# A ring of four tiles for the divided weights in a hybrid mixer block, in place of two tiles set aside for one pair

## The chip, the cores and the metric

The kernel runs on one core of one Trainium2 chip. The metric is the device time of one execution in microseconds, the median of several runs. Names of engines: PE is TensorE (PEld its weight loads, which may overlap with the matmuls), DVE is VectorE, ACT is ScalarE, POOL is GpSimd, and SP issues most of the DMAs.

## The reference

One block for 512 tokens of width 1024: a norm, one wide projection, four sequence mixers side by side, gates, an output projection, and a feed-forward part with a short convolution. Everything is float32.

```python
D_MODEL = 1024; SEQ = 512; MIX_WIDTH = 512; D_FF = 2816
u = rms_norm(h, mix_norm_g[l])
fa, fb, fc, fd, fg = _split(u @ w_in[l], MIXER_IN_SIZES)
branches = (rwkv7_mix(fa, ...), gla_mix(fb, ...), mlstm_mix(fc, ...), ssd_mix(fd, ...))
gates = jax.nn.sigmoid(fg).reshape(bsz, t, N_BRANCH, D_MODEL)
merged = gates[:, :, 0] * (branches[0] @ branch_proj[l, 0])
for i in range(1, N_BRANCH):
    merged = merged + gates[:, :, i] * (branches[i] @ branch_proj[l, i])
h = h + merged @ w_out[l]
u = rms_norm(h, ffn_norm_g[l])
gate, val = _split(causal_dwconv(u @ ffn_up[l], ffn_conv_w[l], ffn_conv_b[l]), (D_FF, D_FF))
h = h + (jax.nn.silu(gate) * val) @ ffn_down[l]
return rms_norm(h, final_norm_g)
```

Of the four mixers, `rwkv7_mix` is a recursion with a matrix state of 64x64 per head, `gla_mix` a gated linear attention with 4 heads, `mlstm_mix` a gated attention with a convolution ahead of it, and `ssd_mix` a state space model in chunks of 128 tokens.

## The kernel before

**Dense work.** A float32 operand is divided into a part `hi` that TensorE takes at its fast rate (type F32R) and the rest, `lo`. A product is three matmuls: `hi` by `hi`, `hi` by `lo`, `lo` by `hi` (`mm3`, lines L232 to L234; L327 to L329 where tokens are the output's rows). Activations are divided once (`uh`, `ul` and their like). Weights come from HBM in halves of 128x512 (`raw`, three tiles). For each half ACT copies `raw` to `hi` (L222), and DVE or, for some, POOL subtracts to get `lo` (L223). Both parts live in rings of three tiles each (`w_tiles`, L215, pool `wp`). Each output tile of 128x512 collects eight blocks of 128 in PSUM, from a ring of three (`psd`); an L899, for instance, reads it for the convolution of mLSTM, in three steps by the three earlier tokens, and the last one frees the tile.

**Mixers.** Between the dense matmuls stand the small ones of the mixers, in plain float32: L810, L821, L835, L847, L851 of the gated linear attention (L821 makes the chunks' contributions to the state, 64x128 from 32 rows; L835 the scores within a chunk, 32x32 from 64 rows), L626 to L687 of the rwkv recursion, L1002 to L1060 of the state space model. In the rwkv part, DVE inverts triangular matrices of 32x32 in 31 steps of two instructions (`Mt` L597, `Mi` L599), twice in the program (two halves of heads); the result goes to DRAM and comes back in another layout as `MN` and `MT` (L600 to L613). L626 needs `MN`, L631 needs `MT`; then eight chunks follow one another through L650, L661, L663 (DVE), L673, L687 (TensorE) and the state `st` (DVE).

**The feed-forward part.** `fm_halves` computes two output tiles at once, one of the gate and one of the value, from four halves of weights. The weights of the first pair are wanted while the last work of the part before still goes on. Three of its four halves use the rings, the fourth two tiles of their own, `wxh` and `wxl`, in a pool `hw` that is closed right after.

**What sets the order.** The code is written stage by stage, but the order on each engine is set by the framework: a list scheduler goes through all instructions with a model of their times, and takes at each point what is ready by that model, by a priority. `split_h` gives the divide a raised priority (`tc.high_priority`). A tile of a ring counts as free once its last reader is done, so the number of tiles decides when a divide counts as ready, and with that what comes next on every engine. After that the order is fixed; on the chip each engine takes its instructions in that order and waits on semaphores.

Of the kernel before, what the change touches and what calls it, by code (L numbers as in the profile page):

```python
# [10 lines left out]
F32R = mybir.dt.float32r  # L11
# [5 lines left out]
P = 128  # L17
# [143 lines left out]
def kernel(ctx: ExitStack, tc: tile.TileContext, A, out):  # L161
# [22 lines left out]
    wp = ctx.enter_context(tc.tile_pool(name="wp", bufs=1))  # L184
# [7 lines left out]
    def pd():  # L192
        return dense[0].tile([P, T], F32, tag="d", name="psd")
# [18 lines left out]
        return pf[lo:hi, PF_AT[name] + i:PF_AT[name] + i + 1]  # L212

    def w_tiles():
        return (wp.tile([P, 512], F32R, tag="hi", name="hi", bufs=3), wp.tile([P, 512], F32R, tag="lo", name="lo", bufs=3))  # L215

    def split_h(src, h, tiles=None, eng=V):
        raw = wp.tile([P, 512], F32, tag="raw", name="raw", bufs=NRAW)
        nc.sync.dma_start(raw, src[:, 512 * h:512 * h + 512])
        hi, lo = tiles or w_tiles()  # L220
        with tc.high_priority(Q["split"]):
            S.copy(hi, raw)  # L222
            eng.tensor_tensor(lo, raw, hi.bitcast(F32), op=ALU.subtract)  # L223
        return hi, lo
# [3 lines left out]
    def split_w(src, tiles=(None, None), eng=V):  # L228
        return [split_h(src, h, tiles[h], G if (pl[0] >> h) & 1 else eng) for h in range(2)]

    def mm3(ps, lh, ll, rh, rl, first, last):
        PE.matmul(ps, lh, rh, start=first, stop=False)  # L232
        PE.matmul(ps, lh, rl, start=False, stop=False)  # L233
        PE.matmul(ps, ll, rh, start=False, stop=last)  # L234
# [36 lines left out]
    def fm_halves(jobs, eng=V):  # L271
        ws = [split_w(src, tiles, eng) for src, tiles in jobs]
        pss = [pd() for _ in jobs]
        for h in range(2):
            ts = slice(256 * h, 256 * h + 256)
            for w, ps in zip(ws, pss):
                for k in range(KD):
                    hi, lo = w[k // 4]
                    ks = slice((k % 4) * P, (k % 4 + 1) * P)
                    mm3(ps[:, ts], hi[:, ks], lo[:, ks], uh[:, k, ts], ul[:, k, ts], k == 0, k == KD - 1)  # L280
        return pss
# [919 lines left out]
    nc.sync.dma_start(gb2, A["gvec"][D:2 * D].partition_broadcast(P))  # L1201
    gb3 = hp.tile([P, D], F32, name="gb3")
    nc.sync.dma_start(gb3, A["gvec"][2 * D:3 * D].partition_broadcast(P))
    hw_ctx = ExitStack()
    hw = hw_ctx.enter_context(tc.tile_pool(name="hw", bufs=1, side="right", reuse_waits="tile"))
    wx = [hw.tile([P, 512], F32R, name=n) for n in ("wxh", "wxl")]
    hx = ExitStack()
    np_ = hx.enter_context(tc.tile_pool(name="nq", bufs=1, side="right", reuse_waits="tile"))

# [18 lines left out]
        norm_T(h2[:, b], gb2, b, np_, uh, ul, 1, [pr_, pm])  # L1228
    tap("h2", h2)
    hx.close()  # L1230
    first = fm_halves([(A["up"][0], (None, None)), (A["up"][1], (None, (wx[0], wx[1])))])
    hw_ctx.close()
    wo_ctx.close()
    mo_ctx.close()
    ps_ctx.close()
# [91 lines left out]
```

## Time and profile before

| | us |
|---|---|
| Median of 3 runs | 1225.39 |
| Lowest and highest run | 1217.79, 1230.0 |
| Profiled execution, its own time | 1220.7 |
| Its span, first to last instruction | 1218.9 |
| TensorE busy in it (share of span) | 1166.5 (96%) |
| VectorE, ScalarE, GpSimd busy | 653.7, 445.5, 333.1 |
| Mean granted clock of TensorE | 0.981 |

Busy times are sums over the span. A busy TensorE is not a TensorE at its peak: a matmul's record reaches from its start to a modelled end, and neighbours overlap. Where records overlap, the distance from start to start tells what an instruction takes of the engine. A matmul in plain float32 leaves two records.

### The profile page before, as it was taken

The page shows a single profiled execution, that of the slowest core. Times are in us where ns is not written, and L with a number is a line of the kernel's source. Part 1 is how long each engine was busy: PE and PEld are TensorE (multiplying, and loading weights), DVE is VectorE, ACT ScalarE, POOL GpSimd, SP SyncE. Part 2 cuts the span into 40 slices and gives each one's busy share as a digit, 9 for nine tenths or more (in the row PEclk, how much of TensorE's full clock was granted, in tenths as well). Part 3 has the DMA queues.
Part 4 walks back from the last instruction along what each step waited for, and adds up shares of the span by engine and source line. Part 5 has one row for each costly group of instructions (what it writes and reads, how often), then busy time and mean ns, then how long its engine had stood idle before and what let it go on. Part 6 is the DMA issues. An engine that isn't in the chain of part 4 may idle for free.

```text
span 1218.9 us, 17897 instructions
## 1 busy us (share of the span) xinstructions
PE 1166.5 (96%) x6881; PEld 935.6 (77%) x6881; DVE 653.7 (54%) x1090; ACT 445.5 (37%) x820; POOL 333.1 (27%) x287
## 2 busy tenths in 40 slices
PE   5999989999999998989999999999999999999997
PEld 4886865777779965767877877778888888888886
DVE  5257792444675437397224654464556656562323
ACT  4355232223322533223123434342444444442323
POOL 3113110023473246241112363440122222220100
PEclk9998987999999999999999999999999999999999
DMA  5122330122332221323123532463222322323232
GB/s 203 62 88 65 83 85 25 36 83 83 97 104 70 95 90 65 81 78 109 60 72 105 190 112 87 164 217 87 79 95 95 103 96 96 95 95 100 92 102 104
DMA packets 79886, 117.30 MB, mean 96 GB/s; under 512 B 22660, under 2 KB 27172, under 8 KB 79800
## 3 DMA queue, kind: packets, MB, share of 16 engines
q1 hardware_dynamic: 79224, 115.11, 29.7%
q8 instruction: 54, 0.88, 0.3%
q10 hardware_dynamic: 576, 1.05, 0.2%
q14 instruction: 32, 0.26, 0.1%
HBM read 107.93 MB, written 8.19 MB: 95 GB/s over the span
## 4 chain that ended last, share of the span: by engine, by line
PE 74%; DVE 10%; DMA 7%; issue 4%; POOL 2%; ACT 2%; SPq 0%; POOLq 0%; DVEq 0%; ACTq 0%
PE psd L232 16%; PE psd L233 16%; PE psd L234 15%; PE psd L1276 3%; PE psd L1274 3%; PE psd L1275 3%; DVE Mt L597 2%; DVE Mi L599 2%; PE psd L328 2%; PE psd L327 2%; PE psd L329 2%; DVE lo L223 2%; DMA sab<-ad 2%; PE psr L673 1%; DMA raw<-in_wo_dram 1%
## 5 line engine op out<-in xcount | busy, mean ns | idle before, releaser
L223 DVE TENSOR_TENSOR lo<-raw,hi 128x512 fp32r<-128x512 f32 x280 | 226.7, 811 | 299.9 <-ACT hi L222 285.0
L222 ACT CAST hi<-raw 128x512 fp32r<-128x512 f32 x322 | 199.4, 620 | 495.6 <-PE psd L233 300.7
L232 PE MATMUL psd<-uh,hi 128*128 128x512 f32 (+1 forms) x912 | 364.0, 400 | 15.0 <-ACT hi L222 5.1
L234 PE MATMUL psd<-uh,lo 128*128 128x512 f32 (+1 forms) x912 | 362.7, 398 | 5.4 <-DVE lo L223 4.2
L233 PE MATMUL psd<-ul,hi 128*128 128x512 f32 (+1 forms) x912 | 360.5, 396 | 0.2 <-DVE ul L249 0.2
L232 PEld LDWEIGHTS psd<-uh,hi 128*128 128x128 f32 x912 | 173.3, 190 | 57.0 <-ACT hi L222 7.3
L234 PEld LDWEIGHTS psd<-uh,lo 128*128 128x128 f32 x912 | 173.4, 190 | 48.8 <-DVE lo L223 6.2
L233 PEld LDWEIGHTS psd<-ul,hi 128*128 128x128 f32 x912 | 173.4, 190 | 37.3 <-issue 3.1
L223 POOL TENSOR_TENSOR lo<-raw,hi 128x512 fp32r<-128x512 f32 x42 | 57.1, 1360 | 245.8 <-ACT hi L222 176.0
L1263 POOL TENSOR_TENSOR y<-y 128x512 f32<-128x512 f32 x22 | 28.3, 1288 | 172.3 <-DVE y L1257 158.4
L1257 DVE SCALAR_TENSOR_TENSOR y<-psd,pf,y 128x510 f32<-128x510 f32 x88 | 65.8, 749 | 3.0 <-issue 0.3
L1276 PE MATMUL psd<-hi,al 128*128 128x512 f32 x164 | 63.8, 389 | 0.0
L1275 PE MATMUL psd<-lo,ah 128*128 128x512 f32 x164 | 63.8, 389 | 0.0
L1274 PE MATMUL psd<-hi,ah 128*128 128x512 f32 x164 | 57.3, 389 | 0.0
L328 PE MATMUL psd<-lo,uh 128*128 128x256 f32 x192 | 56.1, 292 | 1.0 <-DVE lo L223 1.0
L327 PE MATMUL psd<-hi,uh 128*128 128x256 f32 x192 | 55.5, 289 | 0.0
L329 PE MATMUL psd<-hi,ul 128*128 128x256 f32 x192 | 55.4, 289 | 0.0
L328 PEld LDWEIGHTS psd<-lo,uh 128*128 128x128 f32 x192 | 37.0, 193 | 5.0 <-issue 3.2
L327 PEld LDWEIGHTS psd<-hi,uh 128*128 128x128 f32 x192 | 36.9, 192 | 1.9 <-issue 1.3
L329 PEld LDWEIGHTS psd<-hi,ul 128*128 128x128 f32 x192 | 37.0, 193 | 1.3 <-issue 1.0
L1275 PEld LDWEIGHTS psd<-lo,ah 128*128 128x128 f32 x164 | 30.8, 188 | 6.4
L1276 PEld LDWEIGHTS psd<-hi,al 128*128 128x128 f32 x164 | 30.8, 188 | 6.4
(418 smaller groups left out, 1725.6 us busy)
## 6 DMA issues: line engine op xcount, KB each, us to landing
raw<-in_wfm_dram SPq DMA_DIRECT2D x140, 256.0 KB, 2.6
raw<-in_up_dram SPq DMA_DIRECT2D x88, 256.0 KB, 2.5
raw<-in_dn_dram SPq DMA_DIRECT2D x44, 256.0 KB, 2.5
raw<-in_bp_dram SPq DMA_DIRECT2D x32, 256.0 KB, 2.6
raw<-in_wtm_dram SPq DMA_DIRECT2D x24, 256.0 KB, 2.6
raw<-in_wo_dram SPq DMA_DIRECT2D x16, 256.0 KB, 2.7
gd<-th SPq DMA_DIRECT2D x15, 256.0 KB, 2.1
th<-gd SPq DMA_DIRECT2D x15, 256.0 KB, 3.0
```

What stands on the lines that cost most here:

```text
L222: S.copy(hi, raw)
L223: eng.tensor_tensor(lo, raw, hi.bitcast(F32), op=ALU.subtract)
L232: PE.matmul(ps, lh, rh, start=first, stop=False)
L233: PE.matmul(ps, lh, rl, start=False, stop=False)
L234: PE.matmul(ps, ll, rh, start=False, stop=last)
L327: PE.matmul(o, uh[:, k, bs], hi[:, cs], start=first, stop=False)
L328: PE.matmul(o, uh[:, k, bs], lo[:, cs], start=False, stop=False)
L329: PE.matmul(o, ul[:, k, bs], hi[:, cs], start=False, stop=last)
L1257: V.scalar_tensor_tensor(y[:, d:T], ps[:, 0:T - d], col("fcw", k * 44 + n), y[:, d:T], op0=ALU.mult, op1=ALU.add)
L1274: PE.matmul(ps, ah[:, k, bs], hi, start=(k == 0), stop=False)
L1275: PE.matmul(ps, ah[:, k, bs], lo, start=False, stop=False)
L1276: PE.matmul(ps, al[:, k, bs], hi, start=False, stop=(k == NF - 1))
```

## The change

The two rings get four tiles each, and the pool `hw` goes; the fourth half of the first up pair takes its tiles from the rings like the others.

```diff
     def w_tiles():
-        return (wp.tile([P, 512], F32R, tag="hi", name="hi", bufs=3), wp.tile([P, 512], F32R, tag="lo", name="lo", bufs=3))
+        return (wp.tile([P, 512], F32R, tag="hi", name="hi", bufs=4), wp.tile([P, 512], F32R, tag="lo", name="lo", bufs=4))
...
-    hw_ctx = ExitStack()
-    hw = hw_ctx.enter_context(tc.tile_pool(name="hw", bufs=1, side="right", reuse_waits="tile"))
-    wx = [hw.tile([P, 512], F32R, name=n) for n in ("wxh", "wxl")]
     hx = ExitStack()
...
-    first = fm_halves([(A["up"][0], (None, None)), (A["up"][1], (None, (wx[0], wx[1])))])
-    hw_ctx.close()
+    first = fm_halves([(A["up"][0], (None, None)), (A["up"][1], (None, None))])
```

No instruction that computes is added or removed. The scheduler's order changes on all engines from the first mixers on. TensorE's dense matmuls stand in the same order among themselves; the small ones stand at other places between them. Groups of small matmuls between dense ones were 189 and are 141.

TensorE, before, in the gated linear attention of its second pair of heads (`psm_2026` and `psm_2027` are two PSUM tiles that L821 fills, `psd_2276` is a dense output tile):

```order
L821 MATMUL psm_2027<-w_1424,w_1907 64x128
L233 MATMUL psd_2276<-ul_85,hi_2272 128x512
L821 MATMUL psm_2026<-w_1425,w_1907 64x128
L234 MATMUL psd_2276<-uh_84,lo_2273 128x512
L821 MATMUL psm_2027<-w_1425,w_1907 64x128
L232 MATMUL psd_2276<-uh_84,hi_2272 128x512
L821 MATMUL psm_2026<-w_1425,w_1907 64x128
L233 MATMUL psd_2276<-ul_85,hi_2272 128x512
L821 MATMUL psm_2027<-w_1425,w_1907 64x128
```

TensorE, after, the same L821 (`MT` is that of the recursion):

```order
L631 MATMUL psr<-MT,Y_926 32x32 x31
L650 MATMUL psr<-vp_615,zm_710 64x64 x3
L673 MATMUL psr<-vp_615,zm_710 64x64 x8
L821 MATMUL psm<-w 64x128 x10
L687 MATMUL psr<-xs,MT 64x64
L821 MATMUL psm<-w 64x128 x4
L687 MATMUL psr<-xs,MT 64x64 x3
L650 MATMUL psr<-vp_615,zm_710 64x64 x4
L821 MATMUL psm<-w 64x128 x2
```

The single L821 between dense matmuls now stand together with steps of the recursion, and no dense matmul is between them.

TensorE, before, some 6 us of dense work later (`psm_2060` and `psm_2061` are filled by L835):

```order
L835 MATMUL psm_2060<-w_1909,w_1910 32x32
L232 MATMUL psd_2321<-uh_84,hi_2311 128x512
L835 MATMUL psm_2061<-w_1909,w_1910 32x32
L233 MATMUL psd_2321<-ul_85,hi_2311 128x512
L835 MATMUL psm_2060<-w_1909,w_1910 32x32
L234 MATMUL psd_2321<-uh_84,lo_2312 128x512
L835 MATMUL psm_2061<-w_1909,w_1910 32x32
L232 MATMUL psd_2321<-uh_84,hi_2317 128x512
```

TensorE, after, the same L835:

```order
L234 MATMUL psd<-uh,lo 128x512
L673 MATMUL psr<-uu,zm_710 64x64 x8
L673 MATMUL psr<-vp_615,zm_710 64x64 x8
L835 MATMUL psm<-w 32x32 x29
L661 MATMUL psr<-st,kr 64x64 x4
L835 MATMUL psm<-w 32x32 x3
L232 MATMUL psd<-uh,hi 128x512
```

All 32 L835 of these two tiles moved into one gap between dense matmuls.

VectorE, before, in the first inverse, where the third L899 (128x511) frees a dense PSUM tile:

```order
L223 TENSOR_TENSOR lo_2183<-raw_2180,hi_2182 128x512
L599 TENSOR_TENSOR Mi_845<-Mi_845,Mt_846 64x10x22
L899 SCALAR_TENSOR_TENSOR w_2166<-psd_2141,pf_77,w_2166 128x509
L597 TENSOR_TENSOR Mt_846<-Ls_842,Mi_845 64x207
L899 SCALAR_TENSOR_TENSOR w_2166<-psd_2141,pf_77,w_2166 128x510
L599 TENSOR_TENSOR Mi_845<-Mi_845,Mt_846 64x9x23
L827 SCALAR_TENSOR_TENSOR w_1779<-w_1778,gdk_1690,w_1779 128x128
L899 SCALAR_TENSOR_TENSOR w_2166<-psd_2141,pf_77,w_2166 128x511
```

VectorE, after, the same place:

```order
L223 TENSOR_TENSOR lo_2183<-raw_2180,hi_2182 128x512
L599 TENSOR_TENSOR Mi_845<-Mi_845,Mt_846 64x12x20
L899 SCALAR_TENSOR_TENSOR w_2166<-psd_2141,pf_77,w_2166 128x509
L597 TENSOR_TENSOR Mt_846<-Ls_842,Mi_845 64x231
L899 SCALAR_TENSOR_TENSOR w_2166<-psd_2141,pf_77,w_2166 128x510
L599 TENSOR_TENSOR Mi_845<-Mi_845,Mt_846 64x11x21
L223 TENSOR_TENSOR lo_2228<-raw_2225,hi_2227 128x512
L899 SCALAR_TENSOR_TENSOR w_2166<-psd_2141,pf_77,w_2166 128x511
```

The third L899 stands behind four steps of the inverse fewer, and the `lo` of the next weight half has come ahead of it.

## Rows read from the trace of the kernel before

**Rows 1.** The page: busy time by engine, and the granted clock in 40 slices.

```profile
PE 1166.5 (96%) x6881; PEld 935.6 (77%) x6881; DVE 653.7 (54%) x1090; ACT 445.5 (37%) x820; POOL 333.1 (27%) x287
...
PEclk9998987999999999999999999999999999999999
```

**Rows 2.** Waits of PE: who waits, for what, us, times, longest.

```profile
PE psd L232 <- ACT hi L222: 5.1, 4, 1.8
PE psd L232 <- DVE w L899: 5.0, 1, 5.0
PE psd L234 <- DVE lo L223: 4.2, 4, 2.5
PE psm L1048 <- DVE sab L1044: 2.4, 1, 2.4
...
PE psr L626 <- DMA MN<-mnd: 1.5, 1, 1.5
...
PE psd L234 <- POOL lo L223: 1.2, 2, 0.8
```

**Rows 3.** Windows: length, busy of PE, PEld, DVE, ACT, POOL; clock, DMA share, GB/s.

```profile
179.20:229.50 50.30, 50.30 (x453) 28.98 (x452) 18.69 (x40) 12.36 (x23) 3.81 (x3) 0.80 0.14 37
179.20:207.20 28.00, 28.00 (x289) 15.81 (x288) 6.73 (x13) 6.72 (x13) 1.52 (x2) 0.74 0.15 37
...
930.00:960.00 30.00, 30.00 (x134) 24.86 (x133) 19.28 (x23) 13.80 (x22) 7.74 (x6) 1.00 0.29 97
324.80:379.10 54.30, 50.18 (x269) 42.43 (x268) 42.17 (x78) 15.39 (x33) 38.65 (x32) 0.97 0.34 94
130.70:174.50 43.80, 38.73 (x299) 31.75 (x298) 42.36 (x102) 14.29 (x26) 7.48 (x5) 0.92 0.19 62
```

**Rows 4.** Lines of PE from 179.2 to 229.5: busy, mean ns, idle.

```profile
L234 PE MATMUL psd<-uh,lo 128*128 128x512 f32 x21 | 11.6, 552 | 0.0
...
L821 PE MATMUL psm<-w 32*64 32x128 f32 x64 | 10.9, 329 | 0.0
L835 PE MATMUL psm<-w 64*32 64x32 f32 x64 | 6.2, 204 | 0.0
```

**Rows 5.** Timeline of PE, L835 in turns: start, duration, instruction.

```profile
211.88 0.25 PE L835 MATMUL psm<-w 64*32 64x32 f32 x2
212.05 0.50 PE L233 MATMUL psd<-ul,hi 128*128 128x512 f32 x1
212.49 0.24 PE L835 MATMUL psm<-w 64*32 64x32 f32 x2
```

**Rows 6.** Timeline of PE, L821 in turns, at full and half clock.

```profile
190.49 0.43 PE L821 MATMUL psm<-w 32*64 32x128 f32 x2
...
191.28 0.43 PE L821 MATMUL psm<-w 32*64 32x128 f32 x2
...
195.38 0.69 PE L821 MATMUL psm<-w 32*64 32x128 f32 x2
...
196.72 0.68 PE L821 MATMUL psm<-w 32*64 32x128 f32 x2
```

**Rows 7.** Timeline of PE, the same two lines in rows.

```profile
146.13 1.10 PE L821 MATMUL psm<-w 32*64 32x128 f32 x32
...
154.18 0.94 PE L835 MATMUL psm<-w 64*32 64x32 f32 x64
```

**Rows 8.** Timeline of PE, L673 at half clock and at full.

```profile
202.69 1.12 PE L673 MATMUL psr<-uu,zm 64*64 64x64 f32 x16
203.60 1.06 PE L673 MATMUL psr<-vp,zm 64*64 64x64 f32 x16
204.60 0.79 PE L233 MATMUL psd<-ul,hi 128*128 128x512 f32 x1
...
221.69 0.63 PE L673 MATMUL psr<-vp,zm 64*64 64x64 f32 x16
222.26 0.25 PE L835 MATMUL psm<-w 64*32 64x32 f32 x2
```

## The prediction

> **What bounds the kernel now.** First the busy times of the page: TensorE (PE) is busy for 1166.5 of 1218.9 us, the next engine for about half [rows 1]. So the end is set by PE's row of work, and a time can change in only two ways: PE waits less or more, or the same matmuls take another time. Second, what PE waits for [rows 2]. The change gives the divided weights one more tile, so the waits for `hi` and `lo` are what it could take away directly: 5.1 + 4.2 + 1.2 = 10.5 us. That is the bound for the obvious effect, under one per cent.
>
> Third, the windows [rows 3]. From 930 to 960 us PE does 134 matmuls in 30.00 us, 0.224 each, at a clock of 1.00 and with no gap. That is what a dense matmul (128x512, lines L232 to L234) costs when nothing disturbs it; there a fourth tile has nothing to give. From 179.20 to 229.50 PE counts as fully busy too, yet it gets through only 61 dense matmuls (21, and 20 for each of the other two lines) and a few hundred small ones [rows 4]. 61 x 0.224 is 13.7 us; the other 36.6 us go to matmuls of 32 and 64 rows and columns (each has two records, so the 64 of L835 are 32 instructions), and to a clock that is 0.74 on average up to 207.2.
>
> The timeline shows why. One L835 and one dense matmul take turns, and each pair takes 212.49 - 211.88 = 0.61 us [rows 5]; less the dense 0.224 that is 0.38 for one L835. Where 32 L835 stand in a row, all of them take 0.94 us, 0.03 each [rows 7]. For L821 a turn takes 191.28 - 190.49 = 0.79 us at full clock and 196.72 - 195.38 = 1.34 at half clock [rows 6], so 0.57 and 1.12 beside the dense; sixteen in a row take 1.10 [rows 7], 0.07 each. What is paid is the alternation.
>
> **A rule weighed against these rows.** The Trainium skill, "Perfetto Trace Analysis", section Identifying the Most-Contended Engine, says that the busy share of matmuls is no good measure of TensorE and that the busy share of weight loads is better. The rows agree: by matmul time the stretch has no idle time and nothing could be won in it, but weight loads are busy for 28.98 of its 50.30 us against 24.86 of 30.00 in the steady one [rows 3]. By the first view the gain there is 0; by the second the stretch, at the steady share, would take 28.98 / 0.829 = 35.0 us, a gain of 15.3. The count of instructions below, which does without this rule, gives somewhat more.
>
> **The change, part by part.** No operation is added or removed: the two extra tiles go, the ring has the same four for the first up pair, and the casts are as many. What the extra tile does before that is to move places, since the scheduler may set a divide earlier. PE's dense matmuls keep their order; the small ones move.
>
> *L835.* In the order of before the 32 of `psm_2060`/`psm_2061` stand one by one between dense matmuls, but for nine; in the new one as 29 and 3. By the timeline 22 gaps hold one L835 alone, so 22 x 0.38 = 8.4 us; in a row these 22 cost 22/32 x 0.94 = 0.7. Gain 7.7.
>
> *L821.* Of the 32 in the stretch, twelve are already together, and 16 stand alone or in twos in 14 gaps: seven at full clock, 7 x 0.57 = 4.0, and seven at half clock, 7 x 1.12 = 7.8, together 11.8. In a row sixteen cost 1.10. Gain 10.7. The seven at half clock rest on the clock's staying up in the new order; if it falls there too, about 7 x 0.5 = 3.5 of it are lost.
>
> *Three gaps with L821 and steps of the recursion* (L687, L650, L673). The 16 L673 of one of them take 204.60 - 202.69 = 1.91 us at half clock; at full clock eight of them take 222.26 - 221.69 = 0.57, so all 1.14 [rows 8]: 0.8. The three L821 in them are worth 0.57 to 1.12 each. 2.5 to 4 in all; I take 3.
>
> Together 21.4 us, with bounds of 17 (the clock still falls, the mixed gaps at their low end) and 22.5.
>
> *New waits in the packed rows.* L687 now has only small matmuls between itself and L631, on which it depends through a copy on ACT; L661 has 29 L835 (0.9 us) between itself and the DVE steps that make `st`. The nearest waits of PE are those of [rows 2], 1 to 2.5 us and once 5.0; there are some seven such dependent steps, most with dense work before them. 0 to 6 us; I take 3, nearer to the cover in the order than to the worst row.
>
> *Weight waits.* 10.5 us at most [rows 2]. `raw` keeps three tiles, and ACT and DVE still serve other chains, so a fourth tile helps only where a divide can start earlier and its engine is free. The long one is a `lo` that stands behind steps of the inverse (`Mt`/`Mi`) on DVE, and the new order sets such a `lo` some steps earlier. Bounds -10.5 to +4 (other places can wait instead); I take -2.
>
> *L899.* PE waits 5.0 us for the third L899, which frees the PSUM tile [rows 2]; the PSUM ring is unchanged. In the new DVE order that L899 stands behind four steps of the inverse fewer, while a second `lo` has come ahead of it. A DVE instruction there takes 42.36/102 = 0.42 us on average [rows 3], so 4 x 0.42, less a little: -1.5, with bounds 0 and -5.0.
>
> *The inverse.* With three more L899 in its midst the first chain ends some 4 us later, and its first user L626 stands 5.2 us of dense work later (23 x 0.224): nothing. The second chain has the same, and PE already waits 1.5 us for `MN` behind it [rows 2]: +1, bounds -1.5 to +3.
>
> *The SSD stage.* It comes 22 us of dense work later and has other dense work between its groups: 33 matmuls of half the size where 24 full ones stood, 3.7 us of cover in place of 5.4. PE idles there now for 54.30 - 50.18 = 4.1 us [rows 3], of it 2.4 at L1048 [rows 2]. +2, bounds 0 and +5.
>
> **Sum.** -21.4 + 3 - 2 - 1.5 + 1 + 2 = -18.9 us, against the profiled execution's 1220.7: 1201.8. That execution lies 4.7 below the median of the runs shown, and a median of the new kernel need not lie as low, so I add half of it: 1204.
>
> **Rivals.** (a) *Given back by later waits.* With PE some 20 us earlier at 230 us, the chains on DVE and POOL are not earlier: POOL is busy for 38.65 of 54.30 us in the SSD stage [rows 3], and PE waits there and at `MN` for what the grouping has won. For it: these chains are of other engines and don't get shorter. Against it: after the stretch PE has 100 us of dense work before the SSD stage, in which they can go ahead. It leaves 5 to 10 us of gain: 1212 to 1218. (b) *Alternation is not what costs.* The gaps would then be paid by the small matmuls in whatever order; only the waits for weights and L899 would go, some 5 to 10 us: 1213 to 1218. Against it stand the same instructions in a row at a tenth of the price [rows 7]. (c) *Slower: the packed rows wait.* Small matmuls taken out from between dense ones no longer cover DVE's and ACT's steps. If each of the seven dependent steps of the recursion waited as long as the longest wait, 5.0 us [rows 2], that is 35 us instead of 3, and the time 1236; the point from which it is slower than before is 24 us of waits, 3.5 per step. For it: the clock was at half in this very stretch. Against it: most waits in [rows 2] are under 2.5 us, and in the new order 11 to 20 dense matmuls (2.5 to 4.5 us) stand before most of these steps. The Trainium skill, "Perfetto Trace Analysis", section Optimization Strategy, speaks for this one: it says that mixing stretches bound by different engines may help, and the change unmixes them. By that rule the stretch gets longer; no row here shows it so far. (d) *The fourth tile doesn't change what runs*: only the order on paper. It does change the order, so this has no chance of its own.
>
> **How the numbers follow.** The forecast, 1196 to 1211: 0.72. Rival (a): 0.17. Rival (b): 0.05. Rival (c): 0.06. One per cent of the median, 12.3 us, is about what a measurement of this kernel can tell from no change, its three runs being 12 us apart. Below 1213.1 lie the forecast and a part of (a): faster 0.76. Within: the rest of (a), (b) and a little of (c): 0.19. Slower: 0.05. The range: at the low end the forecast less 6 more of the weight waits and 4 of L899 and `MN`, some 1194; at the high end it takes in (a) and (b), 1217.
>
> **What would show it.** Right: dense matmuls from 170 to 230 us of the new profile at a steady pitch, L835 and L821 as rows of some ten and more instructions of about 1 us, PEclk at 9 in the slices that now show 7 and 8 [rows 1], and the dense matmul that ended at 229.5 ending some 18 us earlier. The terms of waits: L232 for L899 about 3.5 in place of 5.0; waits for `hi` and `lo` about 8; new lines for L687, L661 or L673 of 1 to 2 us each; L1048 about 4. From 930 us on nothing changes. Wrong: if the groups of L835 cost as much as the single ones did; if the half clock stays in the stretch in spite of the grouping; or if the lead is gone by the time of the SSD stage, which a comparison of the start of the first up pair in both traces shows.

## The result and the profile after

The changed kernel takes 1203.49 us (median, 1199.54 to 1205.4) against 1222.29 for the kernel before (1217.79 to 1230.0): a ratio of 0.9844, with a 95% interval from 0.9809 to 0.9879. It is faster by about 19 us, and the interval is clear of no change. Its profiled execution took 1205.4 us with a span of 1203.6, so 15.3 less than the profiled execution before; stages are compared in these two.

The page of the changed kernel: busy times and the clock.

```profile
PE 1148.7 (95%) x6881; PEld 935.0 (78%) x6881; DVE 653.1 (54%) x1090; ACT 443.9 (37%) x820; POOL 335.0 (28%) x287
...
PEclk9998989999998999998999999999999999999999
```

The number of matmuls is the same, 6881, and yet PE is busy for 17.8 us less [rows 1]. What PE stands idle has not shrunk: 1218.9 - 1166.5 = 52.4 us before, 1203.6 - 1148.7 = 54.9 after. So the change did not win its time by waiting less, which is what a further buffer is usually for. The slice in which the clock stood at 7 is gone.

Waits of PE in the changed kernel (who waits for what: us in total, times, longest).

```profile
PE psd L232 <- DVE w L899: 4.8, 3, 3.8
PE psr L626 <- DMA MN<-mnd: 4.5, 1, 4.5
PE psr L565 <- DVE bk L530: 3.4, 2, 2.0
...
PE psr L661 <- DVE st L705: 2.8, 1, 2.8
PE psr L1060 <- DVE sbt L1042: 2.7, 1, 2.7
PE psd L232 <- DVE y L1253: 2.1, 1, 2.1
...
PE psd L234 <- DVE lo L223: 1.5, 2, 0.8
```

The waits for weights, 10.5 us in [rows 2], are down to 1.5; as much has come up elsewhere, at `MN`, `bk`, `st`, `sbt` and `y`.

To compare stage with stage, take dense matmuls that both kernels do in the same order, and the time at which each starts. They are numbered by how much dense work stands ahead of them, in matmuls of 512 columns. Number 480 starts at 179.25 before and 185.75 after, number 608 at 259.95 and 244.33. Windows of the changed kernel: from the 480th to the 608th; steady; and the last quarter of the first up pair with most of the second pair.

```profile
185.75:244.33 58.58, 55.74 (x690) 45.69 (x689) 30.25 (x59) 20.49 (x39) 9.32 (x6) 0.97 0.24 67
912.00:942.00 30.00, 30.00 (x135) 24.82 (x134) 18.04 (x22) 13.84 (x22) 7.73 (x6) 1.00 0.29 97
840.77:856.77 16.00, 13.93 (x69) 11.79 (x67) 8.37 (x13) 8.37 (x13) 2.56 (x2) 0.89 0.30 98
```

The same two stretches of the kernel before.

```profile
179.25:259.95 80.70, 80.70 (x751) 55.40 (x750) 28.65 (x61) 21.17 (x40) 10.15 (x7) 0.87 0.14 40
859.99:872.10 12.11, 12.11 (x69) 10.57 (x67) 7.49 (x11) 7.58 (x11) 2.58 (x2) 1.00 0.21 73
```

From the 480th to the 608th dense matmul the changed kernel needs 58.58 us instead of 80.70: 22.1 less, the whole gain and more, with the clock at 0.97 instead of 0.87. In the steady stretch nothing changed (30.00 us for 135 matmuls). At the end of the first up pair it loses 3.9 us.

Two things share in the 22.1 us beside the order within the window. The changed kernel's window holds 61 matmul records fewer (690 for 751): steps of the recursion now stand behind the 608th dense matmul, where PE's timeline gives them some 2 us. And the half clock is part of it: by the clocks of the two windows, 80.70 x 0.13 less 58.58 x 0.03 is 8.7 us, an estimate that takes the half clock as doubling the time and so an upper one (a turn of L821 goes from 0.79 to 1.34 us).

The timeline of PE in the changed kernel, at the two groups that [rows 5] and [rows 6] show in turns.

```profile
201.14 0.87 PE L821 MATMUL psm<-w 32*64 32x128 f32 x20
...
206.68 0.39 PE L234 MATMUL psd<-uh,lo 128*128 128x512 f32 x1
207.00 0.68 PE L673 MATMUL psr<-uu,zm 64*64 64x64 f32 x16
207.52 0.63 PE L673 MATMUL psr<-vp,zm 64*64 64x64 f32 x16
208.08 0.71 PE L835 MATMUL psm<-w 64*32 64x32 f32 x58
211.62 0.45 PE L661 MATMUL psr<-st,kr 64*64 64x64 f32 x8 [2.83 <-DVE st L705]
```

29 L835 (58 records) take 0.71 us, where each of 22 cost 0.38 before. Behind them stands the price that was forecast as a new wait: L661 has nothing left to cover DVE's step for `st` and waits 2.83 us.

| Stretch, by the start of the same dense matmul | before | after | difference |
|---|---|---|---|
| start to the 480th | 179.25 | 185.75 | +6.5 |
| 480th to the 608th | 80.70 | 58.58 | -22.1 |
| 608th to the 1421st (gates, SSD, start of the second recursion) | 256.10 | 250.19 | -5.9 |
| 1421st to the 1881st (second recursion) | 144.01 | 144.56 | +0.6 |
| 1881st to the last quarter of the first up pair | 199.93 | 201.69 | +1.8 |
| from there over most of the second pair | 12.11 | 16.00 | +3.9 |
| from there to the end | 346.80 | 346.83 | 0.0 |

The differences add up to the -15.3 of the two spans, rounding aside.

### The profile page after: what moved, and what is told of

It reads as the page before. It is cut to its first block, busy times and chain, and to the rows that moved or that the text cites. A ratio compares the mean times of both kernels' runs of the same rounds, so it can differ in the third digit from the quotient of the medians.

```text
span 1203.6 us, 17896 instructions
## 1 busy us (share of the span) xinstructions
PE 1148.7 (95%) x6881; PEld 935.0 (78%) x6881; DVE 653.1 (54%) x1090; ACT 443.9 (37%) x820; POOL 335.0 (28%) x287
## 5 line engine op out<-in xcount | busy, mean ns | idle before, releaser
L232 PE MATMUL psd<-uh,hi 128*128 128x512 f32 (+1 forms) x920 | 361.3, 395 | 9.5 <-DVE w L899 4.8
L234 PE MATMUL psd<-uh,lo 128*128 128x512 f32 (+1 forms) x920 | 360.1, 393 | 1.5 <-DVE lo L223 1.5
L232 PEld LDWEIGHTS psd<-uh,hi 128*128 128x128 f32 x920 | 174.5, 190 | 49.8 <-issue 9.5
L234 PEld LDWEIGHTS psd<-uh,lo 128*128 128x128 f32 x920 | 174.6, 190 | 39.3 <-DVE lo L223 2.4
L1253 DVE SCALAR_TENSOR_TENSOR y<-psd,pf,y 128x510 f32<-128x510 f32 x88 | 65.6, 746 | 2.6
L1270 PE MATMUL psd<-hi,ah 128*128 128x512 f32 x164 | 63.8, 389 | 0.0
L328 PE MATMUL psd<-lo,uh 128*128 128x256 f32 x192 | 57.3, 298 | 0.0
L328 PEld LDWEIGHTS psd<-lo,uh 128*128 128x128 f32 x192 | 38.8, 202 | 2.2 <-issue 1.8
L1270 PEld LDWEIGHTS psd<-hi,ah 128*128 128x128 f32 x164 | 30.8, 188 | 6.4
```

Source lines behind the costliest of these rows:

```text
L328: PE.matmul(o, uh[:, k, bs], lo[:, cs], start=False, stop=False)
L1253: V.scalar_tensor_tensor(y[:, d:T], ps[:, 0:T - d], col("fcw", k * 44 + n), y[:, d:T], op0=ALU.mult, op1=ALU.add)
L1270: PE.matmul(ps, ah[:, k, bs], hi, start=(k == 0), stop=False)
```

## The experiments

Three questions: is it the grouping or the tile; what makes a turn dear; and why is time lost at the first up pair.

**Grouping without the tile.** Three tiles and the two extra ones, all as before; L821 and L835 alone get a raised priority, so that the scheduler sets each group in one piece.

```diff
                 psu = [pm(), pm()]
-                for b in range(NB):
+                with tc.high_priority(800):
+                    for b in range(NB):
...
             psa = [pm(), pm()]
-            for b in range(NB):
+            with tc.high_priority(800):
+                for b in range(NB):
```

> Three tiles and the two extra ones as before, but L821 and L835 get a raised priority, so that in the order all 32 L835 and the L821 of each PSUM pair stand together. Theory A (grouping is the gain): 21 us less in that stretch, some of it given back or not by the rest of the new order: 1204, from 1197 to 1211. Rival B (the fourth tile takes away waits for weights): the tiles are those of before, so 1222, from 1216 to 1227.

Measured: 1205.61 us (1203.08 to 1207.35), a ratio of 0.9876, interval 0.9815 to 0.9937, against 1223.17 before. The window of this kernel from the 480th to the 608th dense matmul, and PE's timeline in it.

```profile
181.99:239.42 57.43, 57.43 (x692) 47.26 (x691) 29.45 (x58) 21.03 (x39) 10.44 (x7) 0.94 0.18 51
```

In this kernel L822 and L837 are the lines that were L821 and L835.

```profile
200.21 1.10 PE L822 MATMUL psm<-w 32*64 32x128 f32 x32
...
207.76 0.76 PE L837 MATMUL psm<-w 64*32 64x32 f32 x64
```

With not one tile added, the stretch takes 57.43 us, even less than in the changed kernel, and the whole time falls by about as much. The waits for weights are nearly those of before: 2.9 us for `hi` and 5.9 for `lo` on L234, against 5.1 and 5.4.

```profile
PE psd L234 <- DVE lo L223: 4.7, 5, 2.4
PE psd L232 <- ACT hi L222: 2.9, 3, 1.8
...
PE psd L234 <- POOL lo L223: 1.2, 2, 0.8
```

Rival B, that the tile wins by the waits that it takes away, expected 1222 and falls.

**One tile alone.** The change for `hi` only, and for `lo` only. The edit of the first, against the changed kernel (line shortened); the second puts the 3 at `hi`.

```diff
-wp.tile([P, 512], F32R, tag="lo", name="lo", bufs=4)
+wp.tile([P, 512], F32R, tag="lo", name="lo", bufs=3)
```

> The change with four tiles for hi alone; lo keeps three. In the order of it L821 stands grouped and 16 of the 22 single L835 remain single, and three L851 become single in addition. Theory A: the L821 gain of 10.7 and the half clock's 3, with 2 from L835, less 1 for L851: about 13 less, 1209, from 1203 to 1215. Rival B (waits for weights): only the waits for hi (5.1 us) can go, so 1217 to 1222.

> The change with four tiles for lo alone; hi keeps three. On TensorE and VectorE the order up to the first up pair is that of before, but for a handful of rows. Theory A: same as before, 1222, from 1217 to 1226. Rival B: the waits for lo (5.4 us) go, so about 1217.

Measured: `hi` alone 1213.83 us (1210.04 to 1217.11), ratio 0.9938, interval 0.9913 to 0.9964; `lo` alone 1218.93 (1216.69 to 1226.3), ratio 0.9984, interval 0.9957 to 1.0012. The window from the 480th to the 608th, of `hi` alone.

```profile
181.77:245.75 63.98, 61.73 (x681) 47.61 (x680) 30.99 (x62) 20.62 (x39) 10.40 (x7) 0.97 0.23 61
```

The same window of `lo` alone.

```profile
177.69:258.30 80.61, 80.61 (x752) 55.19 (x750) 29.53 (x61) 21.31 (x40) 10.15 (x7) 0.87 0.14 40
```

With a fourth `lo` alone the order stays, and the stretch stays with it (80.61 against 80.70). Its time can't be told from that of the kernel before, though its interval just reaches the 5 us of the rival; but the waits that the rival counted on did not go: L234 still waits 4.2 us for `lo` from DVE and 1.4 from POOL. With a fourth `hi` alone, L821 is grouped and 16 L835 still stand in turns, and the stretch is in between, at 63.98: 16.7 less than before. The whole kernel won only 8 to 9 (0.6% by the ratio, 9.3 us by the medians): it came out near the upper end of what was expected, and more was given back further on. PE waits 4.8 us for `th` on ACT in six waits and 4.6 on DVE in three, against 1.0 and 1.8 before, and once 3.2 for `lo` at L328.

**One group alone.** Three tiles, with the raised priority for L821 only and for L835 only (one half of the first diff each).

> Three tiles, raised priority for L821 alone. In the order L821 is grouped; 15 L835 remain in turns with dense matmuls, and nine L847 and L851 have come into turns. Theory A: 15 x 0.38 less what they cost in a row = 5.3, and 9 x 0.14 to 0.23, so 6.5 to 7 us above the kernel with both grouped: 1212, from 1206 to 1217. Rival B: 1222, as with three tiles in the kernel before.

> Three tiles, raised priority for L835 alone. In the order L835 is grouped; seven L821 remain in turns. Theory A: 7 x 0.50 at full clock or 7 x 1.05 at half clock above the kernel with both grouped: 1209 to 1213. Rival B: 1222.

Measured: 1207.11 us (1202.23 to 1219.1), ratio 0.9874, interval 0.9818 to 0.993, for L821 alone; 1210.49 (1205.96 to 1218.47), ratio 0.989, interval 0.9854 to 0.9926, for L835 alone. The windows from the 480th to the 608th, first of the kernel with L821 grouped.

```profile
182.54:254.41 71.87, 71.87 (x755) 53.53 (x754) 29.94 (x60) 21.34 (x40) 10.57 (x7) 0.83 0.16 44
```

Then of the one with L835 grouped.

```profile
182.29:247.31 65.02, 65.02 (x692) 50.71 (x691) 28.82 (x58) 21.31 (x39) 9.45 (x7) 0.87 0.19 50
```

Both lie between 57.43 and 80.70, so each group carries a part, and rival B falls for both. With L821 alone grouped the stretch is 14.4 us longer than with both, twice the 6.5 to 7 expected for the 15 L835 and the nine L847 and L851 in turns. The L835 stand where the clock is at half (0.83 over the window), and there a turn takes 0.97 us, as the timeline of that kernel shows (its L836 was L835); some 2 us are recursion steps that lie inside this window and not in the other (755 records for 692).

```profile
206.80 0.31 PE L836 MATMUL psm<-w 64*32 64x32 f32 x2
207.77 0.31 PE L836 MATMUL psm<-w 64*32 64x32 f32 x2
208.73 0.31 PE L836 MATMUL psm<-w 64*32 64x32 f32 x2
```

The whole times follow the stretch only roughly. By the medians of each comparison L821 alone won 16.3 us and L835 alone 12.9, although the second has the shorter stretch by 7. The medians less the stretch differ by up to 13 us among the three kernels with grouping and three tiles, and the intervals of the two overlap. The profiled run of L835 alone is also the slowest of its seven, 8 us above their median.

**What a turn costs.** A kernel of matmuls alone, held in a given order: a dense one and one or more small float32 ones in turns, then the small ones in a row. It leaves out the whole block. A second kernel does the same with other shapes.

```diff
+    def turns(small, k=1):
+        for i in range(24):
+            dense()
+            for j in range(k):
+                small(i * k + j)
```

> Leaves out the whole block and measures only rows of matmuls: dense 128x512 ones alone, then in turns with one small matmul, then the small ones in a row. Theory A (the alternation is what costs): the float32 matmul of 64 rows by 32 columns costs about 0.38 us per turn beside the dense 0.22, and 32 of them in a row about 1 us; four of them per turn cost hardly more than one (0.45). If the change of the array's shape makes the price, a float32 matmul over the full 128x128 array in turns costs clearly less, 0.12. The 32-row one of 64 columns costs about 0.57 per turn. Rival B (the price belongs to the small matmul, whatever stands beside it): the price per small matmul is the same in a row and in turns, and four per turn cost four times as much.

> Leaves out the whole block and measures turns of a dense matmul with one small float32 matmul of 32 columns of output: on 64 rows by 32 columns of the array, on 64 rows by all 128 columns, on all 128 rows by 32 columns, and on 64 by 64 with 64 columns of output; then turns with two and with eight of the first kind. Theory A (a change of the array's shape is what a turn pays, once in and once out): all of the first four pay 0.3 to 0.5 us beside the dense one, and two or eight per turn pay hardly more than one (0.39 and 0.45). If only the split of the rows counts, the 128x32 one pays no more than the 0.23 of a full 128x128 one. Rival B (each small matmul has its price): two per turn pay 0.76, eight 3.0.

Measured, from the distance of one turn to the next less the 0.22 of the dense matmul, at full clock:

| Small matmul, part of the array (rows x columns) | in turns, each | in a row, each |
|---|---|---|
| 64x32 (L835's shape), one per turn | 0.38 | 0.02 |
| the same, two, four, eight per turn | 0.39, 0.40, 0.43 a turn | |
| 128x32 | 0.39 | |
| 64x64 | 0.46 | |
| 64x128 | 0.54 | |
| 32x64 with 128 columns of output (L821's shape) | 0.57 | 0.07 |
| 128x128, the full array, float32 | 0.23 | 0.22 at full clock (0.26 with its end at half clock) |

PE's timeline in the second kernel, with one L835-like matmul per turn and with eight (two records each).

```profile
23.64 0.24 PE L53 MATMUL small<-raw 64*32 64x32 f32 x2
...
24.24 0.24 PE L53 MATMUL small<-raw 64*32 64x32 f32 x2
...
160.20 0.29 PE L53 MATMUL small<-raw 64*32 64x32 f32 x16
...
160.85 0.29 PE L53 MATMUL small<-raw 64*32 64x32 f32 x16
```

0.60 us from one to the next with one, 0.65 with eight. A turn has one price, whatever the number in it; theory A holds and rival B falls. On the full array a small float32 matmul costs the same in turns (0.23) and in a row (0.22), so the type isn't what is paid for; the 0.12 expected for it was too low. A part of the rows or of the columns is enough: 64x128 pays and 128x32 pays, where 0.23 was the other possibility for the second; what these two cost in a row was not measured. This fits what the Trainium skill, "TensorEngine Tiling (Array Packing)", section Key Properties, says: that changing the tiling mode drains TensorE. The runs show a price, not the drain itself: for the two shapes measured both ways it is 0.36 and 0.50 us per turn, in and out together.

The same kernels show the clock. In the first one, windows of dense matmuls alone, of turns with 64x32, early and late, and of the full-array float32 matmuls in a row, with no other engine at work and PE never idle.

```profile
10.50:23.50 13.00, 13.00 (x48) 10.53 (x47) 0.00 (x0) 0.00 (x0) 0.00 (x0) 1.00 0.00 0
25.20:34.00 8.80, 8.80 (x42) 4.51 (x40) 0.00 (x0) 0.00 (x0) 0.00 (x0) 0.92 0.01 2
34.00:38.50 4.50, 4.50 (x16) 2.33 (x15) 0.00 (x0) 0.00 (x0) 0.00 (x0) 0.50 0.00 0
...
86.00:92.00 6.00, 6.00 (x50) 6.00 (x49) 0.00 (x0) 0.00 (x0) 0.00 (x0) 0.88 0.01 3
```

The first row is dense matmuls alone. (Up to 15.2 us they still start 0.43 us apart, the pace of dense ones at the half clock, though the column says 1.00; from there on it is 0.23.) Some 9 us into the turns the granted clock falls from full to half, with nothing to wait for. So a half clock like the one that made the worst part of [rows 3] worse can come in the midst of turns, without any idle time. It doesn't follow each time: 24 turns with 128x32, with 64x64, with the full array, or with two, four or eight of 64x32 per turn kept 1.00. Nor does it need turns: the last row is small float32 matmuls in a row, and there too the clock falls to half. What decides it these runs don't show.

**The first up pair.** In the built program of the changed kernel, the first up pair sits in PSUM banks 0 and 1, and the next tile gets bank 0 again; so its first matmul waits for the second L1253, which reads the gate there, and on DVE a `lo` stands ahead of that L1253. In the kernel before the pair sat in banks 1 and 2, and the next tile's bank 0 was free. Two edits were tried. The first passes over two tiles.

```diff
     dense[0] = psf
+    for _ in range(2):
+        pd()
```

> The changed kernel with two PSUM tiles passed over when the feed-forward part begins, so that its second pair starts in a bank that nobody reads any more, not in that of the first pair's gate. Theory: TensorE's 2.1 us wait for L1253 and the half clock after it (about 1.8 us) go: 3.9 us less than the changed kernel, 1199.6, from 1196 to 1203. Rival: the wait only moves on to the divide of the next weights, whose hi and lo are not earlier: 1203.5.

Measured: 1203.29 us (1199.37 to 1208.77), the changed kernel's time, and L232 still waits 2.1 us for `y`. In the built program a tile that nobody writes takes no bank, and the next one still got bank 0. This edit tells nothing about the cause; it is a second measurement of the changed kernel (ratio 0.9827, interval 0.9784 to 0.9869). The second edit writes one column, so that the bank is taken.

```diff
     dense[0] = psf
+    V.memset(pd()[:, 0:1], 0.0)
```

> The changed kernel with one PSUM tile of the feed-forward part used up by a memset of one column, so that in the built program its second pair gets bank 7, not the gate's bank 0, and its first matmul waits for ACT alone. Theory: the 2.1 us wait for L1253 and the 1.8 us of half clock after it go: 3.9 us less than the changed kernel, 1199.5, from 1196 to 1203. Rival: another wait takes its place, 1203.4.

Measured: 1197.36 us (1197.11 to 1203.61) against 1218.88 before; ratio 0.9827, interval 0.9798 to 0.9857. The window of this kernel that answers to 16.00 us above.

```profile
836.49:848.60 12.11, 12.11 (x68) 10.58 (x67) 7.60 (x12) 8.10 (x12) 2.58 (x2) 1.00 0.26 87
```

12.11 us, as before the change, at a clock of 1.00: the bank was the cause of the wait and of the half clock after it. On DVE the order is still that of the changed kernel, a `lo` ahead of the second L1253, so it was not this. By the trace these are 3.9 us. The ratios to the kernel before, 0.9827 and 0.9844, can't tell the two kernels apart.

**Both together.** Four tiles, the raised priority, and the two tiles passed over (which, as above, does nothing).

> Four tiles, raised priority for L821 and L835, and the two PSUM tiles passed over. Theory A (the grouping is the gain, and four tiles have it already): the priority adds little, a few single matmuls fewer; 1199, from 1193 to 1206. Rival B (tiles and grouping are separate gains that add up): 18 us below the changed kernel, 1186.

Measured: 1210.25 us (1207.37 to 1217.97), ratio 0.9893, interval 0.9854 to 0.9932: neither theory's time, and slower than the change alone. The window from the 480th to the 608th, and one of a later stretch, of this kernel.

```profile
184.40:239.63 55.23, 55.23 (x699) 46.55 (x698) 31.02 (x63) 20.94 (x40) 6.79 (x6) 1.00 0.25 66
...
370.00:462.00 92.00, 79.13 (x378) 63.36 (x378) 40.90 (x72) 33.78 (x66) 41.93 (x35) 0.91 0.21 65
```

The stretch is the best of all, 55.23 us at a clock of 1.00. More than what was won there is lost behind it: from the 608th to the 1296th dense matmul, which take in the SSD stage, this kernel needs 222.6 us and the changed one 206.2. In the second window PE is idle for 12.9 us: it waits 5.7 for L421, 2.5 and 1.6 for `sab` and `sbt` of the SSD stage, 2.5 for L478, where the changed kernel has no wait between the 1047th and the 1296th; and the clock is at 0.91. Which change of the order brings these waits was not settled, and this profiled run is the slowest of its six, 7.7 us above their median. Rival B falls; that the priority adds little holds for the stretch alone.

**Three tiles, grouped, with the bank taken.**

> Three tiles, L821 and L835 grouped by priority, and the same memset. Its first pair had the same clash of banks, with a wait of 1.5 us and the clock at 1.00. Theory: 1.5 to 1.8 us less than without the memset, 1203.9, from 1199 to 1208; so that three tiles with the grouping come within some 5 us of four tiles with the same memset. Rival B (tiles are the gain): 1222.

Measured: 1202.08 us (1194.55 to 1204.94), ratio 0.9848, interval 0.9817 to 0.9878. The wait of 1.5 us at the first pair is gone from this kernel's trace. Three tiles come as far as four, if the order has its small matmuls together. The fastest median is that of four tiles with the bank taken, 1197.36; by the intervals it is not clear of this one.

## Why the prediction was right

The time, 1203.49, came out at the forecast's 1204, and the main mechanism is shown: the stretch, the alternation in it and the price of a turn. By the profiled executions the forecast was -18.9 us and -15.3 came. That the median hit 1204 to within 1 us is in part luck: the misses below go both ways and nearly cancel. The terms, one by one:

- *L835, L821 and the mixed gaps*, -21.4 forecast. The stretch from the 480th to the 608th fell by 22.1 with 2.8 of new waits in it, so 24.9 without them: 3.5 more than forecast. Some 2 us of that are the recursion steps that left the window, which is no gain.
- *New waits in the packed rows*, +3 forecast: L661 waits 2.8 us for `st`, and the other dependent steps hardly anything. Right in size and place. Rival (c) needed 3.5 us at each of seven steps; one had 2.8. Unmixing did no harm: the Trainium skill's advice to mix stretches with different bounds ("Perfetto Trace Analysis", Optimization Strategy), on which that rival drew, is not borne out by this stretch, which went from 80.70 to 58.58 us. But both kinds of matmul in it are TensorE's own; of stretches bound by different engines it shows nothing.
- *Weight waits*, -2 forecast: they fell from 10.5 to 1.5, by 9. This term was mis-sized; the bound of 10.5 was nearly reached. But other waits rose by as much, so that PE's idle time went from 52.4 to 54.9.
- *L899*, -1.5: the longest wait for it is 3.8 us instead of 5.0, about as forecast; but two short ones came up, and with them the sum is 4.8, hardly less than before.
- *The inverse*, +1: the wait for `MN` grew from 1.5 to 4.5 us, the upper bound, while the second recursion's stretch grew by 0.6 only; the wait of 2.5 us for `lo` in it went.
- *The SSD stage*, +2: L1048 and L1060 wait 3.8 us together (0.7 + 0.4 + 2.7), against 2.4. The whole stretch that holds it got 5.9 shorter.
- *The first up pair*, forecast at nothing ("the ring has the same four"). It lost 3.9 us. The count of tiles was the same, but the order on DVE and the bank were not; the kernel with the memset shows both the cause and that it can be had back.
- *Before the 480th dense matmul*, not forecast: 6.5 us lost. The same 1022 matmul records stand ahead of it in both kernels, so no work moved into this part. PE is idle there for 24.0 us instead of 20.2, and busy for 161.7 instead of 159.1, at a mean clock of 0.94 instead of 0.96. The waits that grew are those at the start (by 0.6), of L565 for `bk` (2.0, none before), of L546 (1.7 for 0.4) and for `ul` (1.6 for 0.9). Which change of the order brings them was not tested.

Rivals (a) and (b) fall: the lead of some 16 us at the 608th dense matmul was never under 12.8 us behind the SSD stage and was 19.2 at the start of the first up pair (849.86 before, 830.64 after), and alternation is what costs. The estimate by the share of weight loads (-15.3) pointed to the right stretch but was too small, against 22 to 25; that it equals the difference of the two whole spans is chance.

## What to carry to other kernels

Where one engine is the bound, look for stretches in which it is called busy and gets little done, by dividing the time by what the same instruction costs in an undisturbed stretch. On TensorE, keep matmuls that use a part of the array together, and don't set them one by one between full ones: here a turn cost 0.4 to 0.6 us, and a whole group 1 us. Where a scheduler sets the order, a change of a buffer's count is a change of the whole order; read what it did to the order before you credit the buffer, and expect each new order to bring waits and bank clashes of its own.

## What was not expected of the hardware

A turn's price does not depend on how many small matmuls are in it: 0.60 us from turn to turn with one, 0.65 with eight. Small float32 matmuls over the whole array pay no such price, 0.23 us in turns and 0.22 in a row. And in turns of a dense matmul with one of 64x32 the granted clock can fall to half, with PE at work all the time: 1.00 in the dense part, 0.50 some 9 us into the turns; it did not with two or more of 64x32 per turn.
